# RG-LRU stage in a fixed order on three engines, with GpSimd's products and weight splits on VectorE and one convolution tap on ScalarE

## The chip, the cores and the metric

The kernel runs on 1 core of one Trainium2 chip. The time is device microseconds of one execution. Lower is better.

The engines are named as in the profile: PE is TensorE (matmuls), DVE is VectorE, ACT is ScalarE, POOL is GpSimd, SP is SyncE, whose queue issues most of the DMAs.

## The reference

A trunk of two layers over 128 prompt tokens and 1024 sample tokens (1152 columns in all, width 1024, inner width 2048). Layer 0 mixes by a Fourier transform, layer 1 by a bidirectional RG-LRU. The change touches layer 1, which is, cut to what matters:

```python
def _centred_dwconv(u, w, b):            # CONV_W = 4 taps per channel
    out = b
    for k in range(CONV_W):
        out = out + up[:, k:k + S] * w[k]

def _rglru_dir(u, w_r, b_r, w_i, b_i, lam, h0, reverse):
    r = sigmoid(_blockdiag(u, w_r) + b_r)          # 8 heads of 256 channels
    i = sigmoid(_blockdiag(u, w_i) + b_i)
    log_a = -LRU_C * r * softplus(-lam)
    a = exp(log_a)
    bterm = sqrt(-expm1(2.0 * log_a)) * (i * u)
    h = scan(a, bterm, reverse)                    # h[t] = a[t] h[t-1] + bterm[t]

def _layer(x, ...):
    u, z = split(h @ w_in, 2)
    uc = _centred_dwconv(u, conv_w, conv_b)
    y = _rglru_dir(uc, ..., False) + _rglru_dir(uc, ..., True)
    out = (y * silu(z)) @ w_out
    return x + gate * out
```

## The kernel before

The tokens lie along the free dimension, the channels on partitions, so the inner width is 16 channel tiles of 128, numbered m; two of them make one of the 8 heads, h. Every product is a float32 product made of three matmuls with rounded parts: high times high, high times low and low times high (`mm3`, L100 to L103). A float32 tile is split into such parts by `split` (L89): ACT casts the high part, and DVE or another engine subtracts it from the source for the low part. `wload` (L93) loads a 128 x 1024 tile of weights by SP's queue and splits it.

Stage H (from L798) runs over the heads. `stage_a` makes for both tiles of a head the projection u (three PSUM banks of 386, 384 and 388 columns, 24 matmuls each; ACT copies them to SBUF, L842), the convolution `uc` (the first tap with its bias on DVE, L847, then three more taps on DVE, L850) and its parts `uh` and `ul` (L852, recorded at L90 and L91). `stage_g` makes for one tile the two gates of both directions: 36 matmuls each tile and direction, tanh on ACT into `tr` and `ti` (L874), two more functions of `tr` into `nu` and `ga` (L878, L879), the square root (L882), then on DVE a run of products (L884 to L887), on POOL the product `ti*tr` (L888; on DVE in the last head), and on DVE the forward scan (L893), the backward scan (L897) and their sum (L902). POOL copies one column of each scan to `st`, the state that is an output. `z_mm` projects the gate branch z of a tile (72 matmuls) and makes z times its sigmoid in `szz` (L913 on ACT, L914 on DVE), and `z_out` multiplies it with the scans' sum (L919) and stores the result to `gD`, by SP's queue for the tiles up to 13 and by POOL's for 14 and 15. The low parts of the weights of this stage, and of the first weights of the stage after it, are made on POOL.

The output projection (`out_stage`, L682) reads `gD` again, as 16 tiles of 384 columns for each of three chunks (`g_load`, L609: the DMA into `gr`, then `gh` and `gl`), and multiplies it with `w_out`: 48 matmuls for each of 8 output tiles m. The `gr` tile of chunk 0 and channel tile 10 is written gr1010 in the order below, and so on; wo1020h is the high part of the first half of the weights of chunk 0 and output tile 2.

The order in which each engine gets its instructions isn't that of the source: the program is built with a list scheduler that simulates a timeline and places instructions by it. Each engine then works through its own list in order. In matmul order, a head goes: gates of its first tile, z of that tile, gates of its second tile, u of the two tiles of the next head, z of the second tile; then the next head's gates.

## Time and profile before

| | us |
|---|---|
| median of 3 runs | 1561.07 |
| lowest, highest | 1560.8, 1563.4 |
| span of the profiled execution | 1557.0 |
| PE busy | 1476.6 |
| DVE busy | 1105.8 |
| ACT busy | 744.8 |
| POOL busy | 443.3 |

The span is one execution on the hardware profiler, from its first to its last instruction; the time of a run is somewhat longer than the span. Busy times are sums over the instructions of one engine; a row that waits for another engine or for a DMA isn't counted. What counts for the time is the engine that is always busy and the waits of that engine.

### The profile page before, as it was taken

The page shows a single profiled execution, that of the slowest core. Times are in us where ns is not written, and L with a number is a line of the kernel's source. Part 1 is how long each engine was busy: PE and PEld are TensorE (multiplying, and loading weights), DVE is VectorE, ACT ScalarE, POOL GpSimd, SP SyncE. Part 2 cuts the span into 40 slices and gives each one's busy share as a digit, 9 for nine tenths or more (in the row PEclk, how much of TensorE's full clock was granted, in tenths as well). Part 3 has the DMA queues.
Part 4 walks back from the last instruction along what each step waited for, and adds up shares of the span by engine and source line. Part 5 has one row for each costly group of instructions (what it writes and reads, how often), then busy time and mean ns, then how long its engine had stood idle before and what let it go on. Part 6 is the DMA issues. An engine that isn't in the chain of part 4 may idle for free. (4 is left out here: it accounts for less than half of the span.)

```text
span 1557.0 us, 21619 instructions
## 1 busy us (share of the span) xinstructions
PE 1476.6 (95%) x8362; PEld 1426.1 (92%) x8362; DVE 1105.8 (71%) x1533; ACT 744.8 (48%) x1094; POOL 443.3 (28%) x285
## 2 busy tenths in 40 slices
PE   8879999999999999999699999999998999999997
PEld 5468999999999999999699898989898989899996
DVE  6995456898844677676968686868787787877453
ACT  7362334222223545348384746566573828554221
POOL 5676873000001011113434242515143432200000
PEclk9989999999999999999899999999999999999998
DMA  7523657877745665511111121211111111677451
GB/s 263 195 84 119 229 194 271 285 251 243 231 164 171 206 219 187 191 45 41 43 43 57 42 70 43 69 43 56 56 56 57 43 44 65 197 259 244 151 182 56
DMA packets 81625, 212.73 MB, mean 137 GB/s; under 512 B 9345, under 2 KB 40321, under 8 KB 81393
## 3 DMA queue, kind: packets, MB, share of 16 engines
q1 hardware_dynamic: 81170, 210.18, 40.5%
q8 instruction: 65, 1.06, 0.3%
q0 software_dynamic: 352, 1.18, 0.2%
q14 instruction: 38, 0.31, 0.1%
HBM read 171.98 MB, written 39.35 MB: 136 GB/s over the span
## 5 line engine op out<-in xcount | busy, mean ns | idle before, releaser
L439 POOL TENSOR_TENSOR xr<-xr,tab 128x384 f32<-128x384 f32 (+1 forms) x24 | 23.8, 994 | 365.2 <-DMA xr<-xT 357.6
L888 POOL TENSOR_TENSOR ti<-ti,tr 128x1156 f32<-128x1156 f32 x28 | 78.4, 2800 | 138.2 <-DVE ga L889 109.4
L887 DVE SCALAR_TENSOR_TENSOR ti<-ti,uc 128x1156 f32<-128x1156 f32 x32 | 57.6, 1802 | 63.1 <-ACT ti L874 63.1
L90 ACT CAST uh<-uc 128x1156 fp32r<-128x1156 f32 (+2 forms) x18 | 18.9, 1050 | 165.7 <-DVE uc L850 150.0
L133 DVE SCALAR_TENSOR_TENSOR sil1j<-wada,sil 128x1024 bf16<-128x1024 f32 x64 | 77.9, 1218 | 11.0 <-DMA wada<-w_ada 10.9
L884 DVE SCALAR_TENSOR_TENSOR nu<-ga,nu 128x1156 f32<-128x1156 f32 x32 | 60.9, 1902 | 22.4 <-ACT tr L882 22.3
L850 DVE SCALAR_TENSOR_TENSOR uc<-u,tab,uc 128x1156 f32<-128x1156 f32 (+2 forms) x54 | 75.8, 1405 | 1.1
L739 DVE SCALAR_TENSOR_TENSOR x<-o,ada,xr 128x128 f32<-128x128 f32 (+1 forms) x64 | 31.5, 512 | 55.4 <-PE o L103 54.5
L897 DVE TENSOR_TENSOR_SCAN nu<-ga,tab,ti 128x1155 f32<-128x1155 f32 x16 | 68.0, 4251 | 0.5
L90 ACT CAST gh<-gr 128x384 fp32r<-128x384 f32 x80 | 39.8, 511 | 55.6 <-DMA gr<-gD 55.2
L874 ACT ACTIVATE tr<-g,gb 128x386 f32<-128x386 f32 (+1 forms) x96 | 52.2, 582 | 21.8 <-PE g L103 21.7
L91 DVE TENSOR_TENSOR gl<-gr,gh 128x384 fp32r<-128x384 f32 x77 | 40.8, 554 | 29.7 <-ACT gh L90 29.5
L530 ACT CAST uh<-pu 128x256 fp32r<-128x256 f32 (+1 forms) x32 | 12.7, 398 | 89.3 <-PE pu L103 89.1
L531 DVE TENSOR_TENSOR ul<-pu,uh 128x256 fp32r<-128x256 f32 (+1 forms) x32 | 14.4, 452 | 54.5 <-ACT uh L530 54.4
L874 ACT ACTIVATE ti<-g,gb 128x386 f32<-128x386 f32 (+1 forms) x96 | 51.5, 582 | 0.0
L894 POOL COPY st<-nu 128x1 f32<-128x1 f32 x16 | 18.7, 1171 | 114.2 <-DVE nu L893 114.2
L879 ACT ACTIVATE ga<-tr,sm 128x1156 f32<-128x1156 f32 x32 | 43.3, 1352 | 3.3 <-DVE ga L889 3.3
L878 ACT ACTIVATE nu<-tr,sp2p 128x1156 f32<-128x1156 f32 x32 | 43.6, 1363 | 0.5
L886 DVE SCALAR_TENSOR_TENSOR tr<-ga,tr 128x1156 f32<-128x1156 f32 x32 | 43.2, 1351 | 0.6
L919 DVE SCALAR_TENSOR_TENSOR szz<-szz,nu 128x1155 f32<-128x1155 f32 x16 | 42.8, 2675 | 0.5
L646 ACT ACTIVATE sz<-z 128x384 f32<-128x384 f32 x48 | 22.9, 487 | 40.0 <-PE z L103 19.8
L882 ACT ACT_TABLE_LOAD x32 | 41.1, 1283 | 0.6
(1860 smaller groups left out, 5836.7 us busy)
## 6 DMA issues: line engine op xcount, KB each, us to landing
wo<-w_out SPq DMA_DIRECT2D x96, 512.0 KB, 4.4
wada<-w_ada SPq DMA_DIRECT2D x40, 512.0 KB, 4.2
wz<-w_z SPq DMA_DIRECT2D x32, 512.0 KB, 4.2
gr<-gD SPq DMA_DIRECT2D x80, 192.0 KB, 3.8
yD<-y SPq DMA_DIRECT2D x16, 576.0 KB, 5.2
zy<-yD SPq DMA_DIRECT2D x16, 576.0 KB, 6.6
wu<-w_u SPq DMA_DIRECT2D x16, 512.0 KB, 3.5
wg<-w_gate SPq DMA_DIRECT2D x16, 512.0 KB, 3.7
```

The costliest lines, as they stand in the source:

```text
L90: A.copy(hi, src)
L133: V.scalar_tensor_tensor(junk, w, 0.5, sil[:, q, :], op0=ALU.mult, op1=ALU.mult, accum_out=ada[:, layer, mt, q:q + 1])
L850: V.scalar_tensor_tensor(uc[:, lo:hi], u[:, lo + t:hi + t], convw[:, m, t:t + 1], uc[:, lo:hi], op0=ALU.mult, op1=ALU.add)
L874: A.activation(t[:, lo:hi], pt[:, 0:hi - lo], AF.Tanh, scale=0.5, bias=gb2[:, 2 * d + mat, m:m + 1])
L878: A.activation(nu, tr, AF.Tanh, scale=sp2[:, d, m:m + 1], bias=sp2[:, d, m:m + 1])
L879: A.activation(ga, tr, AF.Exp, scale=sm4[:, d, m:m + 1], bias=sm4[:, d, m:m + 1])
L884: V.scalar_tensor_tensor(nu, ga, 1.0, nu, op0=ALU.add, op1=ALU.mult)
L886: V.scalar_tensor_tensor(tr, ga, 1.0, tr, op0=ALU.add, op1=ALU.mult)
L887: V.scalar_tensor_tensor(ti, ti, 1.0, uc, op0=ALU.add, op1=ALU.mult)
L888: (PL if h < 7 else V).tensor_tensor(ti, ti, tr, op=ALU.mult)
L897: V.tensor_tensor_scan(nu[:, 0:L][:, ::-1], ga[:, 0:L][:, ::-1], ti[:, 0:L][:, ::-1], h0[:, 1, m:m + 1], ALU.mult, ALU.add)
L919: V.scalar_tensor_tensor(sz[:, 0:L], sz[:, 0:L], 0.5, y[:, 0:L], op0=ALU.mult, op1=ALU.mult)
```

## The change

In stage H, the order of PE, DVE and ACT is no longer left to the scheduler. The source is rewritten so that each operation is registered with a class `Plan`: its engine, an estimated cost, and the tiles that it reads and writes. `Plan.order` keeps PE's matmuls in the order in which they are registered, computes for every other operation a latest time from that, and then simulates a list schedule; `emit` issues the operations in that order, and the scheduler is told to keep it for these three engines. DMA issues of the stage are in the plan too, but SP and POOL still go by the scheduler.

With it go these edits: the low parts of the stage's weights are made on DVE (`lo` in `load`); the product `ti*tr` is on DVE in every head (`p5`); the first of the four taps, now the one with offset 2, is computed by ACT straight from PSUM, beside its copy (`tap` in `stage_u`), so that DVE has three taps left; the square roots of both directions of a tile stand together (`roots`); `szz` of tile 15 uses the one buffer of the tag `sz` like the others; and all stores of `gD` in layer 1 stand on SP's queue. The arithmetic is the same but for the order of the taps.

```diff
+        def load(src, name):
...
+            def lo():
+                T["lo", n] = wp.tile([128, 1024], F32R, tag="lo", name=name + "l", bufs=4)
+                V.tensor_tensor(T["lo", n], T["raw", n], T["hi", n].bitcast(F32), op=ALU.subtract)
...
+                def tap(p=p, lo=lo, hi=min(hi, GW)):
+                    A.activation(T["uc", m][:, lo:hi], T["ps", p][:, 0:hi - lo], AF.Identity, scale=convw[:, m, 2:3], bias=convb[:, m:m + 1])
...
-                    V.tensor_scalar(uc[:, lo:hi], u[:, lo:hi], convw[:, m, 0:1], convb[:, m:m + 1],
-                                    op0=ALU.mult, op1=ALU.add)
-                    for t in range(1, 4):
...
+            for t in (0, 1, 3):
+                P.add("DVE", c, lambda t=t: tap(t), r=[ut], w=[("uc", m)])
...
-            return [wload(a["w_gate"][h][:, d], f"wg{h}{d}", PL) for d in range(2)]
...
-            for tr, ti, nu, ga in tt:
-                A.activation(tr, nu, AF.Sqrt, scale=0.25)
+            def roots():
+                for n in ns:
+                    A.activation(T["tr", n], T["nu", n], AF.Sqrt, scale=0.25)
+            P.add("ACT", 4.9, roots, r=[("nu", n) for n in ns], w=[("tr", n) for n in ns])
...
-                (PL if h < 7 else V).tensor_tensor(ti, ti, tr, op=ALU.mult)
+                    V.tensor_tensor(ti, ti, T["tr", n], op=ALU.mult)
...
-            w = uw[2] if m == 0 else wload(a["w_z1"][m], f"wz1_{m}", PL)
-            sz = eb.tile([128, GW], F32, tag="tr" if m == MT - 1 else "sz", name=f"szz{m}", bufs=2 if m == MT - 1 else 1)
+                        T["sz", m] = eb.tile([128, GW], F32, tag="sz", name=f"szz{m}", bufs=1)
...
-            q = SY if m < MT - 2 else PL
-            q.dma_start(gD[1][m][:, 0:SP], sz[:, 0:SP])
-            q.dma_start(gD[1][m][:, SP:NT], sz[:, SP + GAP:L])
+                SY.dma_start(gD[1][m][:, 0:SP], T["sz", m][:, 0:SP])
+                SY.dma_start(gD[1][m][:, SP:NT], T["sz", m][:, SP + GAP:L])
...
+        with tc.manual_schedule(engines=ENG):
+            P.emit()
```

Over the whole program DVE has 1443 rows in place of 1399, ACT 1098 in place of 1082 (40 table loads among them in place of 72), POOL 213 in place of 290, SP 571 in place of 567. PE's 8252 rows stay, with some hundred of them in another place, at the start of head 0 and of each head.

First DVE, at the boundary from head 1 to head 2. The digits in `uc4` and `szz3` are the tile; those in `nu31`, `ga31`, `ti31` and `tr31` are the tile and the direction (1 is backward). Before:

```order
L897 SCALAR_TENSOR_TENSOR nu31_7941<-ga31_7942,tab_148,ti31_7892 128x1155
L847 TENSOR_SCALAR uc4_8054<-u4_7973,tab_148 128x1156
L902 TENSOR_TENSOR nu30_7887<-nu30_7887,nu31_7941 128x1155
L850 SCALAR_TENSOR_TENSOR uc4_8054<-u4_7973,tab_148,uc4_8054 128x1156 x3
L834 MEMSET u5_8069 128x2
L835 MEMSET u5_8069 128x1
L91 TENSOR_TENSOR ul4_8056<-uc4_8054,uh4_8055 128x1156
L847 TENSOR_SCALAR uc5_8150<-u5_8069,tab_148 128x1156
L850 SCALAR_TENSOR_TENSOR uc5_8150<-u5_8069,tab_148,uc5_8150 128x1156 x2
L914 SCALAR_TENSOR_TENSOR szz3_8165<-szz3_8165,zz30_8166 128x386
L850 SCALAR_TENSOR_TENSOR uc5_8150<-u5_8069,tab_148,uc5_8150 128x1156
```

The first row is the backward scan of tile 3, and the taps of uc4 and uc5 stand behind it. Of the same place now, in two pieces:

```order
L1084 SCALAR_TENSOR_TENSOR ti31_7986<-ti31_7986,uc3_7473 128x1156
L1074 SCALAR_TENSOR_TENSOR nu30_7880<-ga30_7992,nu30_7880 128x1156
L1016 SCALAR_TENSOR_TENSOR uc4_7771<-u4_7768,tab_148,uc4_7771 128x1156 x3
...
L944 TENSOR_TENSOR wg21l_8166<-wg21_7943,wg21h_8123 128x1024
L1026 TENSOR_TENSOR ul4_8193<-uc4_7771,uh4_8164 128x1156
L1016 SCALAR_TENSOR_TENSOR uc5_8156<-u5_8153,tab_148,uc5_8156 128x1156 x3
L1131 SCALAR_TENSOR_TENSOR szz3_8229<-szz3_8229,zz30_8168 128x386
L1088 TENSOR_TENSOR ti30_7898<-ti30_7898,tr30_7860 128x1156
...
L1026 TENSOR_TENSOR ul5_8237<-uc5_8156,uh5_8232 128x1156
```

The taps and `ul` of both tiles now stand ahead of both scans of tile 3, which follow further down; a weight split and the product `ti*tr` stand among them.

The second place is DVE at the end of the stage, where gated tile 15 (L919 before, L1138 now) is made while the output projection begins. Before:

```order
L890 MEMSET ti151_11768 128x3
L91 TENSOR_TENSOR gl103_11981<-gr103_11978,gh103_11980 128x384
L91 TENSOR_TENSOR gl104_11987<-gr104_11984,gh104_11986 128x384
L897 SCALAR_TENSOR_TENSOR nu151_11817<-ga151_11818,tab_148,ti151_11768 128x1155
L91 TENSOR_TENSOR gl105_11993<-gr105_11990,gh105_11992 128x384
L902 TENSOR_TENSOR nu150_11763<-nu150_11763,nu151_11817 128x1155
L91 TENSOR_TENSOR gl106_11999<-gr106_11996,gh106_11998 128x384
L91 TENSOR_TENSOR gl107_12005<-gr107_12002,gh107_12004 128x384
L919 SCALAR_TENSOR_TENSOR szz15_11849<-szz15_11849,nu150_11763 128x1155
```

And now:

```order
L1096 SCALAR_TENSOR_TENSOR nu150_11773<-ga150_11871,ti150_11791 128x1156
L186 TENSOR_TENSOR gl107_12038<-gr107_12035,gh107_12037 128x384
L1099 SCALAR_TENSOR_TENSOR nu151_11879<-ga151_11874,tab_148,ti151_11906 128x1155
L1131 SCALAR_TENSOR_TENSOR szz15_11938<-szz15_11938,zz151_11881 128x384
L186 TENSOR_TENSOR gl108_12044<-gr108_12041,gh108_12043 128x384
L186 TENSOR_TENSOR gl109_12050<-gr109_12047,gh109_12049 128x384
L1111 TENSOR_TENSOR nu150_11773<-nu150_11773,nu151_11879 128x1155
L1131 SCALAR_TENSOR_TENSOR szz15_11938<-szz15_11938,zz152_11910 128x386
L186 TENSOR_TENSOR wo1020l_12160<-wo1020_12157,wo1020h_12159 128x1024
L186 TENSOR_TENSOR wo1021l_12166<-wo1021_12163,wo1021h_12165 128x1024
L1138 SCALAR_TENSOR_TENSOR szz15_11938<-szz15_11938,nu150_11773 128x1155
```

The forward scan (nu150) stood well ahead of this place before and now stands directly ahead of the backward one, and two splits for the output projection and two weight splits have come ahead of the gated product.

The third place is SP's queue a little later, where the loads of the output projection and the last stores meet. Before:

```order
L95 DMA wo1031_12199<-w_out_1 128x1024
L622 DMA gr126_13314<-gD1_6_107 128x384
L95 DMA wo1040_12262<-w_out_1 128x1024
L622 DMA gr1010_12020<-gD1_10_111 128x384
L622 DMA gr1011_12026<-gD1_11_112 128x384
```

And now:

```order
L190 DMA wo1031_12232<-w_out_1 128x1024
L190 DMA wo1040_12295<-w_out_1 128x1024
L1141 DMA gD1_15_116<-szz15_11938 128x128
L1142 DMA gD1_15_116<-szz15_11938 128x1024
L717 DMA gr1010_12053<-gD1_10_111 128x384
L717 DMA gr1011_12059<-gD1_11_112 128x384
```

The two stores of gated tile 15, which were on POOL's queue, have come directly ahead of gr1010.

## Rows read from the trace of the kernel before

**Rows 1.** The page's first lines: the span, and each engine's busy time, share of the span and instructions.

```profile
span 1557.0 us, 21619 instructions
PE 1476.6 (95%) x8362; PEld 1426.1 (92%) x8362; DVE 1105.8 (71%) x1533; ACT 744.8 (48%) x1094; POOL 443.3 (28%) x285
```

**Rows 2.** PE's waits over the whole span: the waiting matmul's tile and line, the instruction that released it, the sum of such waits in us, how many, the longest.

```profile
PE g L101 <- ACT uh L90: 32.7, 9, 9.4
...
PE g L101 <- DVE szz L914: 4.1, 6, 0.8
```

**Rows 3.** Busy time of each engine in two stretches: the first is one head of stage H from its gates on, the second reaches from the end of the last z to the first matmul on channel tile 10 in the output projection. After the stretch stand its length and the busy us (and instructions) of PE, PEld, DVE, ACT and POOL, then the granted PE clock, the DMA share and GB/s.

```profile
778.00:861.85 83.85, 79.45 (x432) 78.52 (x432) 63.46 (x55) 50.36 (x65) 30.66 (x14) 0.97 0.16 52
...
1332.64:1360.05 27.41, 24.02 (x115) 20.63 (x115) 20.56 (x25) 10.30 (x18) 6.68 (x6) 0.94 0.68 215
```

**Rows 4.** PE's timeline, single matmuls at which a part of the work begins: start, duration, engine, line, operation, tiles; in brackets the idle time before it and its releaser. In order: a wait in the gates of head 0; the first matmul of u2; of u4; the first gate of head 2, and its next after the wait; the gates' other direction; z4, which follows it; the first matmul of the output projection; the first one on its channel tile 10.

```profile
722.87 0.44 PE L101 MATMUL g<-uh,wg01h 128*128 128x386 f32 x1 [2.13 <-ACT ti L874]
...
726.49 0.33 PE L101 MATMUL u<-h1h,wu_2h 128*128 128x386 f32 x1
...
819.37 0.35 PE L101 MATMUL u<-h1h,wu_4h 128*128 128x386 f32 x1
...
857.43 0.34 PE L101 MATMUL g<-uh,wg20h 128*128 128x386 f32 x1
...
861.85 0.57 PE L101 MATMUL g<-uh,wg20h 128*128 128x386 f32 x1 [3.72 <-ACT uh L90]
...
869.50 0.34 PE L101 MATMUL g<-uh,wg21h 128*128 128x386 f32 x1
...
875.93 0.35 PE L101 MATMUL zz<-h1h,wz_4h 128*128 128x386 f32 x1
...
1332.64 0.34 PE L101 MATMUL o<-gh,wo_0h 128*128 128x384 f32 x1
...
1360.05 0.34 PE L101 MATMUL o<-gh,wo_1h 128*128 128x384 f32 x1
```

**Rows 5.** The timelines of DVE, POOL and ACT at the boundary from head 1 to head 2, in order of time; the columns are those of rows 4.

```profile
838.73 2.40 POOL L91 TENSOR_TENSOR wg21l<-wg,wg21h 128x1024 fp32r<-128x1024 f32 x1
838.84 0.06 DVE L890 MEMSET ti<- 128x3 f32 x1 [2.79 <-POOL ti L888]
838.94 4.61 DVE L897 TENSOR_TENSOR_SCAN nu<-ga,tab,ti 128x1155 f32<-128x1155 f32 x1
...
845.51 4.33 DVE L850 SCALAR_TENSOR_TENSOR uc<-u,tab,uc 128x1156 f32<-128x1156 f32 x3
...
851.07 1.36 DVE L91 TENSOR_TENSOR ul<-uc,uh 128x1156 fp32r<-128x1156 f32 x1 [1.09 <-ACT uh L90]
...
852.87 2.41 POOL L91 TENSOR_TENSOR wz_4l<-wz,wz_4h 128x1024 fp32r<-128x1024 f32 x1 [8.51 <-ACT wz_4h L90]
853.15 2.75 DVE L847 TENSOR_SCALAR uc<-u,tab 128x1156 f32<-128x1156 f32 x1 [0.73 <-ACT u L842]
...
860.64 1.16 ACT L90 CAST uh<-uc 128x1156 fp32r<-128x1156 f32 x1 [5.72 <-DVE uc L850]
```

**Rows 6.** DVE's timeline in the last head: the product `ti*tr`, which is on DVE in that head alone, a backward scan, and a weight split.

```profile
1308.17 1.35 DVE L888 TENSOR_TENSOR ti<-ti,tr 128x1156 f32<-128x1156 f32 x1
...
1309.68 2.62 DVE L897 TENSOR_TENSOR_SCAN nu<-ga,tab,ti 128x1155 f32<-128x1155 f32 x1
...
1326.40 1.22 DVE L91 TENSOR_TENSOR wo1010l<-wo,wo1010h 128x1024 fp32r<-128x1024 f32 x1
```

**Rows 7.** Two stretches with the columns of rows 3: one right after a gate's wait, one in the output projection's first microseconds.

```profile
862.00:865.40 3.40, 3.40 (x11) 3.03 (x12) 3.37 (x4) 2.24 (x5) 2.20 (x1) 0.50 0.00 0
...
1336.40:1339.90 3.50, 3.36 (x10) 3.06 (x11) 3.50 (x4) 0.66 (x2) 2.17 (x2) 0.51 0.28 68
```

**Rows 8.** Groups of instructions: two from the six heads between 780 and 1280 us (line, engine, operation, tiles, shapes, count, busy us, mean ns, idle time before them), and the instructions of line 780 in the stage before (duration in ns: lowest, median, highest).

```profile
L847 DVE TENSOR_SCALAR uc<-u,tab 128x1156 f32<-128x1156 f32 x12 | 21.6, 1796 | 4.4 <-ACT u L842 4.4
...
L882 ACT ACT_TABLE_LOAD x24 | 30.8, 1283 | 0.4
...
L780 ACT ACTIVATE h1h<-x,coef x32: 386/556/622, 539.7 to 680.9; 128x384 fp32r<-128x384 f32 x16, 128x128 fp32r<-128x128 f32 x8, 128x256 fp32r<-128x256 f32 x8
```

**Rows 9.** The timelines of DVE and of SP's queue from the last scans of the stage into the output projection; the columns are those of rows 4. The row of SP at 1352.48 begins with the issue of gr1010, the last row with gl1010.

```profile
1322.57 0.76 DVE L885 TENSOR_SCALAR ga<-nu 128x1156 f32<-128x1156 f32 x1
...
1327.54 2.56 DVE L893 TENSOR_TENSOR_SCAN nu<-ga,ti 128x1156 f32<-128x1156 f32 x1
1330.02 1.33 DVE L887 SCALAR_TENSOR_TENSOR ti<-ti,uc 128x1156 f32<-128x1156 f32 x1
...
1339.57 0.54 DVE L914 SCALAR_TENSOR_TENSOR szz<-szz,zz 128x386 f32<-128x386 f32 x1
1340.05 0.55 DVE L91 TENSOR_TENSOR gl<-gr,gh 128x384 fp32r<-128x384 f32 x1
...
1346.19 1.35 DVE L919 SCALAR_TENSOR_TENSOR szz<-szz,nu 128x1155 f32<-128x1155 f32 x1
...
1352.48 2.07 SPq L622 DMA_DIRECT2D gr<-gD  x4
...
1358.94 2.08 DVE L91 TENSOR_TENSOR gl<-gr,gh 128x384 fp32r<-128x384 f32 x4 [2.87 <-ACT gh L90]
```

**Rows 10.** The page's list of DMA issues: tiles, queue, operation, count, KB each, median us from issue to landing.

```profile
gD<-szz SPq DMA_DIRECT2D x14, 512.0 KB, 3.5
```

More of the change, by code (lines that the diff above doesn't have):

```diff
@@ L823, in body @@
         st = ec.tile([128, 2, MT], F32, name="st")
-        def stage_a(h, early={}):
-            out = []
-            for i in range(2):
-                m = 2 * h + i
-                w = uw[m] if h == 0 else wload(a["w_u1"][m], f"wu1_{m}", PL)
+        P = Plan({"raw": 3, "hi": 4, "lo": 4, "u": 1, "uc": 3, "uh": 2, "ul": 2, "tr": 2, "ti": 3, "nu": 3, "ga": 2, "sz": 1, "ps": 8})
+        T = {}
+        wn = [3]
+        for n in range(3):
+            T["hi", n], T["lo", n] = uw[n]
+            P.given(("hi", n))
+            P.given(("lo", n))
@@ new lines, in body, with psum_ops, mm, wproj @@
+        pn = [0]
+        def psum_ops(name, mms, cost, reads):
+            n = pn[0]
+            pn[0] += 1
+            def mm():
+                T["ps", n] = ps(name)
+                mms(T["ps", n])
+            P.add("PE", cost, mm, r=reads, w=[("ps", n)])
+            return n
+        def wproj(n, name, lo, hi):
+            def mms(pt):
+                proj(pt, (T["hi", n], T["lo", n]), lo, hi)
+            return psum_ops(name, mms, 24 * (hi - lo + 32) / 2400, [("hi", n), ("lo", n)])
@@ L830, in stage_a, with given, stage_u, pads @@
+        def given(tile_):
+            n = pn[0]
+            pn[0] += 1
+            T["ps", n] = tile_
+            P.given(("ps", n))
+            return n
+        def stage_u(m, early=None):
+            n = None if m < 2 else load(a["w_u1"][m], f"wu1_{m}")
+            ut = ("nu", -1) if m == 1 else ("u", max(m - 1, 0))
+            def pads():
                 if m == 1:
-                    u = eb.tile([128, NG + 3], F32, tag="nu", name=f"u{m}", bufs=3)
+                    u = T[ut] = eb.tile([128, NG + 3], F32, tag="nu", name=f"u{m}", bufs=3)
@@ L832, in stage_a @@
                 else:
[L833 removed]
+                    u = T[ut] = ea.tile([128, NG + 3], F32, tag="u", name=f"u{m}", bufs=1)
                 V.memset(u[:, 0:2], 0.0)
                 V.memset(u[:, NG + 2:NG + 3], 0.0)
[L836 to L842 removed]
@@ new lines, in stage_u, with cp @@
+            P.add("DVE", 0.12, pads, w=[ut, ("uc", m)])
+            for c, (lo, hi) in enumerate(HC):
+                if (m, c) in early_n:
+                    p = early_n[m, c]
+                elif m < 2:
+                    p = psum_ops(f"u{m}{c}", lambda pt, lo=lo, hi=hi: proj(pt, uw[m], lo, hi), 24 * (hi - lo + 32) / 2400, [("hi", m), ("lo", m)])
+                else:
+                    p = wproj(n, f"u{m}{c}", lo, hi)
+                def cp(p=p, lo=lo, hi=hi):
+                    A.copy(T[ut][:, 2 + lo:2 + hi], T["ps", p][:, 0:hi - lo])
+                def tap(p=p, lo=lo, hi=min(hi, GW)):
+                    A.activation(T["uc", m][:, lo:hi], T["ps", p][:, 0:hi - lo], AF.Identity, scale=convw[:, m, 2:3], bias=convb[:, m:m + 1])
+                P.add("ACT", 0.48, cp, r=[("ps", p)], w=[ut])
+                P.add("ACT", 0.55, tap, r=[("ps", p)], w=[("uc", m)])
+                if m < 2 and c == 1:
+                    conv(m, ut, 0, hi - 1)
@@ new lines, in z_out, with gated, store @@
+        def z_out(m):
+            def gated():
+                sz = T["sz", m]
+                V.scalar_tensor_tensor(sz[:, 0:L], sz[:, 0:L], 0.5, T["nu", 2 * m][:, 0:L], op0=ALU.mult, op1=ALU.mult)
+            def store():
+                SY.dma_start(gD[1][m][:, 0:SP], T["sz", m][:, 0:SP])
+                SY.dma_start(gD[1][m][:, SP:NT], T["sz", m][:, SP + GAP:L])
+            P.add("DVE", 1.36, gated, r=[("nu", 2 * m)], w=[("sz", m)])
+            P.add("SP", 0.2, store, r=[("sz", m)], lat=5.0)
@@ new lines, in body @@
+        early_n = {k: given(t) for k, t in early.items()}
+        gw = gweights(0)
+        stage_u(0)
+        stage_u(1)
+        for h in range(8):
+            if h == 0:
+                stage_z(0)
+            stage_g(h, gw, 0)
+            if h > 0:
+                stage_z(2 * h)
+            z_out(2 * h)
+            stage_g(h, gw, 1)
+            if h + 1 < 8:
+                stage_u(2 * h + 2)
+                stage_u(2 * h + 3)
+            stage_z(2 * h + 1)
+            z_out(2 * h + 1)
+            if h + 1 < 8:
+                gw = gweights(h + 1)
```

276 lines of the change are left out of this document (198 added, 78 removed).

## The prediction

> **What bounds the kernel now.** I first read the busy times: PE, the tensor engine, works 1476.6 of the span's 1557.0 us, and the next engine, DVE, 1105.8 [rows 1]. So only what makes PE wait, or slows its clock, can give time back. The list of PE's waits names what there is in the stage that the change rewrites (stage H, RG-LRU): 32.7 us in nine waits of gate matmuls for ScalarE's cast `uh`, and 4.1 us for the product on `szz` [rows 2]. The table of stretches shows one head: 83.85 us, PE busy for 79.45 of them, at a mean clock of 0.97 [rows 3].
>
> What would a head take if PE never waited? PE's own rows tell. u4, u5 and z3, 72 matmuls each, run from 819.37 to 857.43, or 12.69 us each; the 36 gate matmuls of one tile and direction run from 869.50 to 875.93, 6.43 us [rows 4]. A head is four of the former and four of the latter: 76.5 us.
>
> Next, why the gates wait. A timeline of the other engines across the boundary from head 1 to 2 shows a chain [rows 5]. DVE stands idle for 2.79 us until GpSimd's product `ti*tr` arrives; the backward scan of tile 3 follows, 4.61 us beside a GpSimd split; only then come the conv taps of uc4, its cast `uh`, the first tap of uc5 at 2.75 us beside another split, the other taps, and its `uh` at 860.64. PE restarts at 861.85, after 3.72 us [rows 4]. Two things make the chain late: the order (the taps of the new head stand behind the scan of the old one, and that behind GpSimd), and a stretch of DVE's rows beside GpSimd. Where GpSimd was quiet the same scan took 2.62 us, and the product, on DVE itself, 1.35 us [rows 6]. After the restart the granted clock is 0.50 (1.2 of 2.4 GHz) for 3.4 us, so 1.7 us more are lost [rows 7].
>
> **The change part by part.** *Waits removed in stage H.* From the start of u2 (726.49) to the end of z15 (1332.64) lie 606.2 us [rows 4]. The PE work in it is 14 u and 15 z parts of 12.69 us and 28 gate parts of 6.43 us, 368.0 + 180.0 = 548.0 us; the matmuls and nearly all of their order stay. If no boundary waits, **58.1 us** go. That hangs on three engines keeping up:
>
> *DVE.* It was busy for 63.46 us of a head [rows 3]. It gains six weight splits at 1.22 us (7.3) and four products at 1.35 us (5.4) [rows 6], and loses two first taps, 21.6/12 = 1.8 us each (3.6) [rows 8]. Without any relief that makes 72.6 us; if only the two backward scans of a head shrink, from 4.61 to 2.62, 68.6. Both stay below 76.5, so DVE isn't the bound by volume; what matters is whether the chain at the boundary is in time. The new order puts the taps of uc4 and uc5 ahead of the old head's scans. Counted from the start of u4, u5's last bank is full at 2 x 12.69 = 25.4 us. Its copy and its new tap on ScalarE end near 26.7, three DVE taps (4.33 us [rows 5]) at 31.0, the cast (1.16 us [rows 5]) at 32.2; DVE has two short rows more in that time (some 1.9 us at most, a `szz` or `ga` row and a product), and `ul5` takes 1.36 us [rows 5]: 34.6. PE needs it when z3 is over, at 3 x 12.69 + 0.3 = 38.4. The slack is about 4 us, so I take no wait.
>
> *ScalarE.* It was busy for 50.36 us of a head [rows 3]. The tap that it takes over is not in the trace: three activations from PSUM a tile. The nearest row is an Identity on 128 x 384 and less, 386 to 622 ns [rows 8]; three are 1.2 to 1.9 us a tile, I take the upper end, 3.7 us a head. Rooting both directions together removes four table loads of a head, 4 x 30.8/24 = 5.1 us [rows 8]. The pair now waits until both directions have their `nu`, and what stands behind it on ScalarE, the later copies of the new u, waits with it; eight PSUM banks cover that for PE. ScalarE ends below where it was.
>
> *GpSimd.* Its products and splits in the stage are gone and two one-column copies a tile are left, so it hardly overlaps with DVE.
>
> *The start.* The gates of head 0 now wait for two more splits on DVE (2 x 1.22 us), while the wait of 2.13 us at 722.87 [rows 4] can go: -2.1 to +2.4 us, I take +0.5. For short waits that may stay (buffers of `ga`, `tr`, `nu` that come free just in time) I add 1.0, between 0 and the 4.1 us that `szz` cost [rows 2].
>
> *The tail, where something is given back.* In the output projection the first ten channel tiles are loaded early; the eleventh, gr1010, waits. Before, the last gated product ended at 1347.54, 14.9 us after z15; gr1010 was issued at 1352.48 and its split began at 1358.94 [rows 9]; PE came to it at 1360.05 [rows 4], 27.4 us after z15, having been busy for 24.0 of them [rows 3]. Now two things differ. Both stores of tile 15, which stood on GpSimd's queue, stand on SP's, directly ahead of gr1010, which so can't be issued before the last gated product is over. And that product is later: from the last `ti` product with uc15 on (begun at 1330.02, 2.6 us ahead of z15's end, before [rows 9]; 2.2 ahead by my count of the new order), the new order has on DVE eight products of 1.35 us, two `ga` rows of 0.76, scans of 2.56 and 2.62, three `szz` rows of 0.55, seven `gl` splits of 0.55 and three weight splits of 1.22 [rows 6, 9]: 10.8 + 1.5 + 5.2 + 1.6 + 3.9 + 3.7 = 26.7, with the small fills 27. That ends 25 us after z15, with a wait or two for `gr` loads 26. From gr1010's issue to its split passed 6.46 us [rows 9], the split is 0.55, the store's two issues some 0.7: PE begins tile 10 some 34 us after z15, with no other work in order. So 34 - 27.4 = **6.6 us** are given back; the ends are 30 us (no `gr` waits, a quicker landing) and 38 (slower loads), that is 2.6 to 10.6.
>
> One rule speaks to the clock in this tail. First the rows: at 1336.4 to 1339.9 PE was granted 0.51 though it was busy for 3.36 of 3.5 us, and after the wait of 2.13 us at 722.87 it stayed at 1.00 [rows 4, 7]. The Trainium skill (TensorE: Matmul & The Clock Gate, "Why this matters for your kernels") lays a throughput drop in mid-kernel to idle gaps between bursts of matmuls; by that, a tail broken into short pieces costs no clock, while the first of these rows says that it may. While PE waits for tile 10 a slow clock costs nothing; it would cost if it lasted beyond. The row's price is half of 3.4 us, 1.7, which I take as nothing and keep for the range.
>
> **Sum.** 1557.0 - 58.1 + 0.5 + 1.0 + 6.6 = 1507.0 us of span. The time outside the span, 1561.07 (the median) - 1557.0 = 4.07 us, stays: **1511 us**. Its own range, with the ends of tail, start and clock, is 1505 to 1518.
>
> **The rivals.** *The tail is free* (0.10): the rows between the scans are short, the loads land early and nothing is lost after z15: 1511.0 - 6.6 = 1504.4, 1502 to 1505. Against it stands the store ahead of gr1010.
>
> *A part of each boundary wait remains* (0.16): the slack of 4 us is eaten, by taps from PSUM that take twice as long, by the paired roots holding ScalarE while the new u is ready, or by DVE rows that don't shrink. Waits of 1 to 2.5 us at seven boundaries, with 1.7 us of half clock at the longer ones, make 7 to 29 us: 1518 to 1540. For it: the 3.72 us of before ended a chain of the same kind.
>
> *The stretch is not GpSimd's* (0.05): the scan keeps 4.6 us, DVE has 72.6 us a head in a fixed order, and the chain is late at each boundary as now. Little is left of the 58.1 us: 1545 to 1562. Against it: the scan of 2.62 us [rows 6].
>
> *Slower* (0.06): `szz` has one buffer. ScalarE's tanh into it, at its fixed place, waits until the former tile's store has read it; everything behind it on ScalarE, the tanh of the gates above all, waits too, and PE runs out of PSUM banks. By my count the store is issued some 11 us ahead of that tanh, and such a store landed in 3.5 us [rows 10]. It decides when a store is held up behind a weight load on SP's queue: a buffer free only 23 us after the gated product would cost more than the 7.4 us that a head gains (58.1 over 606.2/76.5 = 7.9 heads), and the kernel is at 1562 or above. All but two of the stores stood on that queue before, which speaks against it.
>
> **How the numbers follow.** Forecast 0.63, free tail 0.10, remaining waits 0.16, stretch 0.05, slower 0.06. The range is 1502 to 1528: it leaves out the upper half of the remaining waits (0.08) and the last two cases (0.11). Within 0.2%, about what a measurement of this kernel can tell from no change, lies 1558 to 1564: the upper part of the stretch case, 0.02. Faster 0.92, slower 0.06.
>
> **What would show it.** Right: no wait of gate matmuls for `uh` above 0.5 us; heads of 76.5 us at clock 1.00; backward scans of 2.6 us throughout; DVE busy for 62 to 69 us a head; z15 over near 1276; in the output projection PE waiting for `gh` or `gl` of tile 10 until some 34 us after that. Wrong: a long wait in DVE's or ScalarE's fixed order behind which ready work stands, PE without free banks, or a store that is late on SP.

## The result, and the profile after

The changed kernel takes 1509.85 us (median of 4 runs, 1507.78 to 1511.16) where the kernel before took 1560.93 in the same session: a ratio of 0.9669, 95% interval 0.9655 to 0.9683. That is 1.2 us from the forecast of 1511 and inside its range. The profiled execution has a span of 1506.0 us. Below, PE is at line 196 to 198 where it was at 101 to 103, and `split` at 185 and 186 where it was at 90 and 91.

The page's first lines, which answer to [rows 1]:

```profile
span 1506.0 us, 21530 instructions
PE 1462.0 (97%) x8362; PEld 1418.6 (94%) x8362; DVE 1084.6 (72%) x1588; ACT 738.6 (49%) x1110; POOL 229.1 (15%) x208
```

PE's waits from 690 to 1400 us (stage H and what follows it), which answer to [rows 2]:

```profile
PE o L197 <- DVE gl L186: 4.4, 3, 1.8
PE o L196 <- ACT gh L185: 2.6, 1, 2.6
PE o L197 <- POOL gl L186: 0.9, 1, 0.9
...
PE g L196 <- ACT ti L1053: 0.6, 1, 0.6
```

Of the gate matmuls (`g`) one waits for 0.6 us, and one for 0.2 us that is not shown, both in head 0; before, they had waited for 32.7 us on `uh`. What is left are waits of the output projection (`o`). Two stretches, in the columns of [rows 3]: a head from u4 to u6, and the time from the end of z15 to the first matmul on channel tile 10.

```profile
800.52:877.00 76.48, 76.48 (x433) 76.45 (x433) 62.85 (x63) 51.13 (x69) 6.52 (x6) 1.00 0.18 57
1272.07:1308.84 36.77, 27.77 (x115) 24.75 (x115) 29.63 (x34) 11.76 (x21) 5.77 (x5) 0.81 0.55 172
```

A head takes 76.48 us and PE is busy in all of it, at full clock. DVE works for 62.85 us of it, less than the 63.46 before, though it has six splits and four products more and only two taps less: its rows are shorter. The second row is the price: 36.77 us where it was 27.41.

The boundary from head 1 to 2 in DVE's timeline, which answers to [rows 5]:

```profile
822.64 1.22 DVE L944 TENSOR_TENSOR wg21l<-wg,wg21h 128x1024 fp32r<-128x1024 f32 x1
823.98 1.36 DVE L1026 TENSOR_TENSOR ul<-uc,uh 128x1156 fp32r<-128x1156 f32 x1
827.18 4.34 DVE L1016 SCALAR_TENSOR_TENSOR uc<-u,tab,uc 128x1156 f32<-128x1156 f32 x3 [1.84 <-ACT u L999]
831.44 0.55 DVE L1131 SCALAR_TENSOR_TENSOR szz<-szz,zz 128x386 f32<-128x386 f32 x1
...
833.50 1.35 DVE L1026 TENSOR_TENSOR ul<-uc,uh 128x1156 fp32r<-128x1156 f32 x1
```

The second `ul` is over at 834.85, 34.3 us after u4's start at 800.52, and PE needs it after 838.59.

Every kernel's profile, those of the experiments too, can be cut at two matmuls: the first of u2, and the last of z15 (its end taken 0.17 us after its start, which is the step from one matmul to the next). The time is the median of the runs; the three columns behind it come from the profiled execution and add up to its span. In us:

| kernel | time | start to u2 | u2 to end of z15 | end of z15 to end of span |
|---|---|---|---|---|
| before | 1560.93 | 726.5 | 606.2 | 224.4 |
| changed | 1509.85 | 724.0 | 548.0 | 233.9 |
| order alone | 1551.55 | 736.7 | 581.5 | 232.2 |
| moves alone | 1504.47 | 727.2 | 548.2 | 224.8 |
| order, GpSimd's work back | 1568.28 | 732.7 | 598.9 | 233.7 |
| tap back on VectorE | 1516.13 | 731.6 | 548.0 | 234.3 |
| product alone | 1533.77 | 726.7 | 578.7 | 224.6 |
| splits alone | 1518.61 | 731.4 | 561.6 | 225.3 |
| stores back on GpSimd's queue | 1512.94 | 727.2 | 548.0 | 235.6 |
| roots of tile 15 apart | 1506.89 | 725.8 | 548.0 | 231.2 |
| product and splits | 1509.86 | 730.9 | 550.7 | 225.8 |
| gl on GpSimd | 1510.15 | 726.0 | 548.0 | 234.8 |
| hybrid | 1502.75 | 724.6 | 548.3 | 227.0 |
| hybrid, tail's edits undone | 1501.42 | 725.6 | 548.2 | 226.6 |

Single numbers of the first column carry some 3 us that aren't the change's: the first gate matmul, ahead of which the compared kernels hardly differ, came at 697.0 to 700.3 us. The second column repeats to a few tenths. The 51.0 us between the spans of the first two rows are 2.4 + 58.1 - 9.5.

One row of the table matters more than the others: the moves alone, in the scheduler's own order, are 5.4 us faster than the changed kernel, and their interval (0.9623 to 0.9652, below) doesn't touch that of the change.

### The profile page after: what moved, and what is told of

It is laid out like the page before. It is cut to its first block, busy times and chain, and to the rows that moved or that the text cites. A ratio compares the mean times of both kernels' runs of the same rounds, so it can differ in the third digit from the quotient of the medians.

```text
span 1506.0 us, 21530 instructions
## 1 busy us (share of the span) xinstructions
PE 1462.0 (97%) x8362; PEld 1418.6 (94%) x8362; DVE 1084.6 (72%) x1588; ACT 738.6 (49%) x1110; POOL 229.1 (15%) x208
## 4 chain that ended last, share of the span: by engine, by line
PE 48%; DVE 2%; ACT 1%; issue 1%; DMA 1%; POOL 0%; DVEq 0%; POOLq 0%; ACTq 0%
PE o L198 4%; PE o L196 4%; PE o L197 4%; PE u L198 4%; PE u L196 4%; PE u L197 4%; PE g L196 4%; PE zz L196 4%; PE zz L198 4%; PE zz L197 4%; PE g L197 4%; PE g L198 4%; DMA gr<-gD 1%; DVE nu L1099 0%; POOL gl L186 0%
## 5 line engine op out<-in xcount | busy, mean ns | idle before, releaser
L228 DVE SCALAR_TENSOR_TENSOR sil1j<-wada,sil 128x1024 bf16<-128x1024 f32 x64 | 78.0, 1219 | 10.8 <-DMA wada<-w_ada 10.6
L1016 DVE SCALAR_TENSOR_TENSOR uc<-u,tab,uc 128x1156 f32<-128x1156 f32 (+2 forms) x54 | 69.2, 1288 | 20.5 <-ACT u L999 19.1
L1097 POOL COPY st<-nu 128x1 f32<-128x1 f32 x16 | 10.4, 648 | 434.0 <-DVE nu L1096 433.7
L1074 DVE SCALAR_TENSOR_TENSOR nu<-ga,nu 128x1156 f32<-128x1156 f32 x32 | 43.5, 1359 | 45.3 <-ACT tr L1070 45.3
L1053 ACT ACTIVATE tr<-g,gb 128x386 f32<-128x386 f32 (+1 forms) x96 | 55.4, 585 | 25.6 <-PE g L198 21.3
L1002 ACT ACTIVATE uc<-u,tab 128x386 f32<-128x386 f32 (+1 forms) x48 | 32.4, 674 | 60.8 <-PE u L198 60.8
L1127 ACT ACTIVATE szz<-zz 128x386 f32<-128x386 f32 (+1 forms) x48 | 23.6, 495 | 74.7 <-PE zz L198 74.5
L1084 DVE SCALAR_TENSOR_TENSOR ti<-ti,uc 128x1156 f32<-128x1156 f32 x32 | 42.9, 1357 | 9.6 <-ACT ti L1053 9.3
L1099 DVE TENSOR_TENSOR_SCAN nu<-ga,tab,ti 128x1155 f32<-128x1155 f32 x16 | 43.9, 2745 | 0.1
L1088 DVE TENSOR_TENSOR ti<-ti,tr 128x1156 f32<-128x1156 f32 x32 | 43.4, 1356 | 0.3
L1096 DVE TENSOR_TENSOR_SCAN nu<-ga,ti 128x1156 f32<-128x1156 f32 x16 | 40.9, 2555 | 0.4
```

The source lines that it names most:

```text
L228: V.scalar_tensor_tensor(junk, w, 0.5, sil[:, q, :], op0=ALU.mult, op1=ALU.mult, accum_out=ada[:, layer, mt, q:q + 1])
L1016: V.scalar_tensor_tensor(T["uc", m][:, lo:hi], T[ut][:, lo + t:hi + t], convw[:, m, t:t + 1], T["uc", m][:, lo:hi], op0=ALU.mult, op1=ALU.add)
L1053: A.activation(T[tg, n][:, lo:hi], T["ps", p][:, 0:hi - lo], AF.Tanh, scale=0.5, bias=gb2[:, 2 * d + mat, m:m + 1])
L1074: V.scalar_tensor_tensor(T["nu", n], T["ga", n], 1.0, T["nu", n], op0=ALU.add, op1=ALU.mult)
L1088: V.tensor_tensor(ti, ti, T["tr", n], op=ALU.mult)
L1099: V.tensor_tensor_scan(nu[:, 0:L][:, ::-1], ga[:, 0:L][:, ::-1], ti[:, 0:L][:, ::-1], h0[:, 1, m:m + 1], ALU.mult, ALU.add)
```

## The experiments

The first question is which of the parts removes the boundary waits. Two theories: the order (the conv taps stood behind the old head's scans), or GpSimd (DVE waited for its product, and was stretched beside it).

**Order alone.** Edit, beside the stores and the square roots as before:

```diff
-                V.tensor_tensor(T["lo", n], T["raw", n], T["hi", n].bitcast(F32), op=ALU.subtract)
+                PL.tensor_tensor(T["lo", n], T["raw", n], T["hi", n].bitcast(F32), op=ALU.subtract)
...
-                P.add("ACT", 0.55, tap, r=[("ps", p)], w=[("uc", m)])
...
+                        PL.tensor_tensor(T["ti", n], T["ti", n], T["tr", n], op=ALU.mult)
```

> The planned order alone: the weight splits and the products ti*tr of heads 0 to 6 back on GpSimd, the first tap back on VectorE from SBUF, the square roots apart, the stores of tiles 14 and 15 back on GpSimd's queue; the planner knows of all that by their costs. Theory 'order' (the gates waited because the conv taps stood behind the old head's scans): most of the gain stays, 1508 to 1520 us. Theory 'GpSimd' (they waited because DVE waited for GpSimd's product and was stretched beside it): more than half of the gain is gone, 1535 us or more, with scans of 4.6 us and waits of gate matmuls for uh or ul of 2 us and more at each boundary.

1551.55 us, ratio 0.9940 (0.9925 to 0.9955). In stage H the order alone wins 24.7 of the 58.1 us, and it loses 10.2 us before u2 and 7.8 in the tail. A wait of 2.7 us stays at each boundary but the first, which has 8.6 us; it is now mostly on `ul`:

```profile
PE g L197 <- DVE ul L1023: 23.7, 9, 4.7
PE g L196 <- ACT uh L1018: 9.4, 2, 6.1
```

At the boundary from head 1 to 2 the backward scan takes 2.62 us, not the expected 4.6; there it is three taps that are long, 8.65 us, beside GpSimd's product and a split.

**Moves alone.** The kernel before with `PL` replaced in the stage's splits and in the product, and the tap on ScalarE:

```diff
-                (PL if h < 7 else V).tensor_tensor(ti, ti, tr, op=ALU.mult)
+                V.tensor_tensor(ti, ti, tr, op=ALU.mult)
...
-            return [wload(a["w_gate"][h][:, d], f"wg{h}{d}", PL) for d in range(2)]
+            return [wload(a["w_gate"][h][:, d], f"wg{h}{d}") for d in range(2)]
...
+                    A.activation(uc[:, lo:min(hi, GW)], pt[:, 0:min(hi, GW) - lo], AF.Identity, scale=convw[:, m, 2:3], bias=convb[:, m:m + 1])
```

> The kernel before with the moves and without the planned order: weight splits and products ti*tr on VectorE, one tap on ScalarE from PSUM, the scheduler's own order. Theory 'GpSimd': the idle time of 2.8 us for the product, 2.0 us of the scan and 1.9 us of the first tap go out of a chain that was 3.7 us late, so most of the gain is there, 1508 to 1522 us. Theory 'order': the scans still stand among the taps and DVE has about 9 us more to do in a head, so the gates still wait 2 to 4 us at each boundary, 1535 to 1560 us.

1504.47 us, ratio 0.9638 (0.9623 to 0.9652), with no planned order at all. A head and the tail, as above:

```profile
804.09:880.57 76.48, 76.48 (x434) 76.45 (x434) 64.13 (x66) 53.46 (x71) 3.96 (x4) 1.00 0.20 65
1275.46:1303.38 27.92, 22.95 (x115) 19.44 (x115) 21.06 (x26) 10.70 (x19) 6.76 (x6) 1.00 0.70 212
```

The head is the same 76.48 us, and the tail is as short as before. At the boundary from head 1 to 2 the scan still stands among the taps of uc4 (one ahead of it, two behind), but its rows have their short lengths:

```profile
822.83 1.42 DVE L850 SCALAR_TENSOR_TENSOR uc<-u,tab,uc 128x1156 f32<-128x1156 f32 x1
...
824.16 2.62 DVE L897 TENSOR_TENSOR_SCAN nu<-ga,tab,ti 128x1155 f32<-128x1155 f32 x1
826.70 1.39 DVE L850 SCALAR_TENSOR_TENSOR uc<-u,tab,uc 128x1156 f32<-128x1156 f32 x1
```

So the planned order isn't needed to remove the waits, and by itself it wins back less than half of what they cost. The scheduler's order isn't quite that of before either (no tap stood ahead of the scan there): it simulates again after every edit, so each run of this kind moves rows too.

**Order, with GpSimd's work given back** (tap and paired roots kept):

```diff
-                V.tensor_tensor(T["lo", n], T["raw", n], T["hi", n].bitcast(F32), op=ALU.subtract)
+                PL.tensor_tensor(T["lo", n], T["raw", n], T["hi", n].bitcast(F32), op=ALU.subtract)
...
+                        PL.tensor_tensor(T["ti", n], T["ti", n], T["tr", n], op=ALU.mult)
```

> The changed kernel with only GpSimd's work given back: weight splits, and the products ti*tr of heads 0 to 6, on GpSimd; tap on ScalarE, paired square roots and planned order kept. Theory 'order': 1506 to 1515 us, no wait of gates above 1 us. Theory 'GpSimd': 1530 us or more.

1568.28 us, ratio 1.0050 (1.0033 to 1.0067): half a per cent slower than the kernel before. Timelines of DVE and POOL at the boundary from head 1 to 2:

```profile
832.52 8.49 DVE L1016 SCALAR_TENSOR_TENSOR uc<-u,tab,uc 128x1156 f32<-128x1156 f32 x3
...
842.67 2.56 DVE L1097 TENSOR_TENSOR_SCAN nu<-ga,ti 128x1156 f32<-128x1156 f32 x1
842.76 4.94 POOL L1109 TENSOR_TENSOR ti<-ti,tr 128x1156 f32<-128x1156 f32 x1 [4.44 <-DVE tr L1080]
...
845.14 3.78 DVE L1026 TENSOR_TENSOR ul<-uc,uh 128x1156 fp32r<-128x1156 f32 x1
848.98 2.62 DVE L1100 TENSOR_TENSOR_SCAN nu<-ga,tab,ti 128x1155 f32<-128x1155 f32 x1
851.52 6.48 DVE L1016 SCALAR_TENSOR_TENSOR uc<-u,tab,uc 128x1156 f32<-128x1156 f32 x3
```

Three taps take 8.49 and 6.48 us in place of 4.34, `ul` 3.78 in place of 1.36. A fixed order doesn't take the stretch away; it lays it on other rows, here the taps that the chain needs. Why this kernel is 17 us slower than the order alone, which lacks the tap on ScalarE and the paired roots among others, no run separates.

**The tap given back** (four DVE taps in the planned order):

```diff
+                V.tensor_scalar(T["uc", m][:, lo:hi], T[ut][:, lo + 2:hi + 2], convw[:, m, 2:3], convb[:, m:m + 1], op0=ALU.mult, op1=ALU.add)
```

> The changed kernel with only the tap given back: the first of four taps on VectorE from SBUF, planned again. DVE has two rows of 0.85 us more in a head, and the chain to ul is 0.85 us longer where 4 us were spare, so both theories say no change, 1508 to 1513 us. A third theory, that the tap on ScalarE carries the gain, says 1525 us or more.

1516.13 us, ratio 0.9712 (0.9696 to 0.9727), above the range of both theories. The heads stay at 76.48 us, as they said; the loss is at the start, where the first gates wait 3.0 us for the split `wg00l`, and some 3 us lie ahead of the first gate, where the runs vary by as much.

The second question: product or splits? Each alone, in the kernel before.

**Product alone:**

```diff
-                (PL if h < 7 else V).tensor_tensor(ti, ti, tr, op=ALU.mult)
+                V.tensor_tensor(ti, ti, tr, op=ALU.mult)
```

> The kernel before with one move: the product ti*tr on VectorE in every head; the weight splits stay on GpSimd, the taps on VectorE, the order the scheduler's. Theory 'wait' (of GpSimd's work it is DVE's idle time for the product that makes the chain late): the 2.8 us before the scan go and 1.35 us of work come, the boundary waits fall below 2 us, 1520 to 1535 us. Theory 'stretch' (it is the longer rows of DVE beside the splits): nearly nothing is won, 1550 to 1562 us.

**Splits alone**, of `wu1` and `wz1` as of `wg`:

```diff
-            return [wload(a["w_gate"][h][:, d], f"wg{h}{d}", PL) for d in range(2)]
+            return [wload(a["w_gate"][h][:, d], f"wg{h}{d}") for d in range(2)]
```

> The kernel before with one move: the stage's weight splits on VectorE; the products stay on GpSimd, the taps on VectorE, the order the scheduler's. Theory 'stretch': the scan falls from 4.6 to 2.6 us and the first tap from 2.75 to 0.85, one or two splits of 1.22 come into the chain, 1520 to 1540 us. Theory 'wait': DVE still stands idle for the product and has 7.3 us a head more to do, 1555 to 1575 us.

The product alone gives 1533.77 us, ratio 0.9826 (0.9812 to 0.9840); the splits alone 1518.61, ratio 0.9730 (0.9716 to 0.9743). One head of each, the product's first:

```profile
855.63:935.30 79.67, 78.12 (x432) 77.52 (x432) 67.11 (x59) 50.28 (x65) 19.40 (x10) 0.98 0.17 55
```

```profile
935.00:1011.50 76.50, 76.50 (x434) 76.33 (x433) 60.91 (x59) 49.91 (x64) 16.66 (x8) 1.00 0.17 58
```

With the splits moved, the heads from the fourth on are already free of waits, though GpSimd still makes the products. In stage H the product alone wins 27.5 us of the 58.1, the splits alone 44.6; together that is more than there is, so the two overlap. They can't be read as the shares of "wait" and "stretch", because each edit mends some of the other's part: with the product alone the backward scans are down to 2.62 us too, and with the splits alone DVE no longer stands idle for the product, as the scheduler has put the first tap of uc4 into that time (beside the product it takes 3.24 us).

**Product and splits, without the tap** (both edits above in one kernel):

```diff
-                (PL if h < 7 else V).tensor_tensor(ti, ti, tr, op=ALU.mult)
+                V.tensor_tensor(ti, ti, tr, op=ALU.mult)
...
-            return [wload(a["w_gate"][h][:, d], f"wg{h}{d}", PL) for d in range(2)]
+            return [wload(a["w_gate"][h][:, d], f"wg{h}{d}") for d in range(2)]
```

> The kernel before with two moves and no more: products ti*tr and weight splits on VectorE; four taps on VectorE, no planned order. If the two moves off GpSimd make the gain, the boundary waits are gone and the time is 1503 to 1512 us. If the tap on ScalarE is needed beside them in the scheduler's order (it takes 1.7 us a head off DVE), waits of 1 to 3 us stay at the boundaries, 1515 to 1530 us.

1509.86 us, ratio 0.9685 (0.9669 to 0.9700): 550.7 us from u2 to z15, so one wait of 1.7 us is left, at the first boundary, and one of 0.4 for `szz`. The tap on ScalarE is worth that and some 2 us at the start.

The third question is the tail. My theory was the store ahead of gr1010; the rival, that the splits `gl` stand behind the late products of tile 15 on DVE.

**Stores back on GpSimd's queue:**

```diff
+                q = SY if m < MT - 2 else PL
```

> The changed kernel with one thing undone: the stores of tiles 14 and 15 on GpSimd's queue, so that no store stands ahead of gr1010 on SP's. Theory 'store' (the prediction's: the tail is long because tile 10 can't be loaded before the last store is issued): tile 10's split comes 5 us or more earlier and the time falls by 4 to 7 us, 1503 to 1506 us. Theory 'chain' (the tail is long because the first splits gl103 to gl107 stand behind the late products and scans of tile 15 on DVE, with half clock after each wait): PE reaches tile 10 no earlier, 1508 to 1511 us.

1512.94 us, ratio 0.9689 (0.9675 to 0.9703), above both ranges; the tail didn't shrink. But the question wasn't put cleanly: without the stores, a third weight load moved ahead of gr1010 on SP's queue, which held it until 1308.21, 33.0 us after z15 in place of 29.5.

**Square roots of tile 15 apart:**

```diff
-            P.add("ACT", 4.9, roots, r=[("nu", n) for n in ns], w=[("tr", n) for n in ns])
+            for g in ([(n,) for n in ns] if m == 15 else [ns]):
```

> The changed kernel with one thing undone: in tile 15 alone the square roots of the two directions stand apart, two table loads more, so that the forward direction's products and scan are over before the last z and not behind it; planned again, which puts the gated product of tile 15 ahead of gl106. Theory 'chain': the waits on gl fall and the gated product ends some 8 us earlier, 1501 to 1506 us, with PE at tile 10 some 28 to 31 us after z15. If the tail is long because the loads gr100 to gr107 themselves come late, it stays at 1508 to 1511 us.

1506.89 us, ratio 0.9652 (0.9639 to 0.9666). The tail is 2.7 us shorter, not 4 to 9: the gated product came 9.5 us earlier, but the output projection's first matmul now waits:

```profile
1279.36 0.69 PE L196 MATMUL o<-gh,wo_0h 128*128 128x384 f32 x1 [5.40 <-ACT gh L185]
```

That cast, of gh100, had its load by 1276.43 and was held until DVE had read uc15 for the last time, in the second `ti` product:

```profile
1278.79 0.51 ACT L185 CAST gh<-gr 128x384 fp32r<-128x384 f32 x1 [2.00 <-DVE ti L1085]
```

The same row holds the second load, gr101, here, in the kernel before and in the changed one. Of the latter, SP's waits from 1255 to 1315 us:

```profile
SPq L717 <- DVE ti L1084: 2.3, 1, 2.3
```

I take it that the output projection's tiles lie where the stage's tiles lay. In this run that row had moved behind the forward scan. gr101 was issued at 1331.38 in the kernel before, 1.3 us ahead of z15's end; at 1273.18 in the changed one, 1.1 us behind it; at 1278.79 here, 5.0 us behind it. In the changed kernel no matmul waited for it, though.

**Low parts gl100 to gl109 on GpSimd:**

```diff
-            gt[0, k] = gt0.get(k) if layer == 0 else g_load(layer, 0, k, None, PL if k in (0,1,2) else V)
+            gt[0, k] = gt0.get(k) if layer == 0 else g_load(layer, 0, k, None, PL if k < 10 else V)
```

> The changed kernel with one thing more: the low parts of the first ten gated tiles of the output projection (gl100 to gl109) on GpSimd, which is idle there, in place of three. Theory 'chain' (splits stand behind tile 15's products on DVE): PE's waits on gl fall from 5.3 to below 3 us and the raw buffers come free earlier, 1505 to 1508 us. Theory 'loads' (the loads gr101 and following can't start before the last reader of uc15 on DVE, whatever engine splits): no change, 1508 to 1511 us.

1510.15 us, ratio 0.9680 (0.9667 to 0.9693): no change. It doesn't decide between the theories, though: PE's waits didn't fall, they only changed their engine.

```profile
PE o L197 <- POOL gl L186: 5.4, 6, 1.9
...
1276.74 11.28 POOL L186 TENSOR_TENSOR gl<-gr,gh 128x384 fp32r<-128x384 f32 x6 [13.17 <-ACT gh L185]
```

GpSimd needs 11.28 us for six of these splits, DVE 0.55 for one; and beside them the rows of tile 15 on DVE are stretched again (a `ti*tr` product 2.15 us in place of 1.35, the backward scan 3.29 in place of 2.62).

**Hybrid**, the planned order up to the last head, then the scheduler's:

```diff
-            P.emit()
+            for i in seq[:cut]:
+                P.ops[i]["fn"]()
+        for i in seq[cut:]:
+            P.ops[i]["fn"]()
```

> The changed kernel with the planned order up to the first gate of the last head; from there on the scheduler sets the order as it did before. If the tail's 9 us are the planned order's (both gate directions of tile 15 in parallel on DVE and ScalarE, so that the rows that free the buffers for gr come late), they go and what is left is 1500 to 1503 us, the fastest of all; if the tail is long for the moves' sake, it stays at 1508 to 1511 us.

1502.75 us, ratio 0.9636 (0.9622 to 0.9649). gr101 is issued 1.6 us ahead of z15's end again, the gated product ends 14.7 us behind it (28.6 in the changed kernel), and the tail is 227.0 us. The stores of tile 15 still stand on SP's queue here.

**Hybrid with the tail's two edits undone:**

```diff
-                        T["sz", m] = eb.tile([128, GW], F32, tag="sz", name=f"szz{m}", bufs=1)
+                        T["sz", m] = eb.tile([128, GW], F32, tag="tr" if m == MT - 1 else "sz", name=f"szz{m}", bufs=2 if m == MT - 1 else 1)
...
+                q = SY if m < MT - 2 else PL
```

> The kernel of the run before (planned order up to the last head, then the scheduler's) with two more edits of the change undone: the stores of tiles 14 and 15 on GpSimd's queue, szz of tile 15 in a buffer of tr. If these two hold the 2.3 us that its tail was still longer than the tail of the kernel before (223.6 in place of 221.3 us from the end of z15 to the end), the time is 1499 to 1502 us; if they don't matter, 1501 to 1504 us.

1501.42 us, ratio 0.9626 (0.9613 to 0.9639): the lowest median of all, and faster than the changed kernel beyond both intervals, but not to be told from the hybrid (0.9622 to 0.9649) or the moves alone (0.9623 to 0.9652). Its tail is 0.4 us shorter than the hybrid's, too little to tell whether these edits matter. (Counted as in the table, the two tails that the expectation compares are 227.0 and 224.4 us.)

## Why the prediction was right, and where it wasn't

*The sum.* 1511 for 1509.85 is closer than its terms were: the tail cost 2.9 us more than forecast, the start 2.9 less, and of the 1.0 us for short waits nothing came. That these cancel is luck. So is it that the 4.07 us "outside the span" did no harm: it is a median less the span of one execution. In the changed kernel the profiled execution took 1507.78 us with a span of 1506.0, so 1.8 us lie outside, and the rest of the difference of 3.85 is that this execution was the quickest of the four.

*What bounds.* Right. PE bound, with the boundary waits to be won; the 58.1 us of stage H came out at 58.1 (606.2 to 548.0), and heads at 76.48.

*Why the gates waited.* I named two causes, the order and the stretch beside GpSimd, and asked the planned order to make room. **This step was half wrong.** The moves alone remove the waits in the scheduler's order; the order alone leaves 33.5 of the 58.1 us, and with the tap and the paired roots but GpSimd at work 50.9. What the order does add is slack: `ul` was ready 34.3 us after u4's start, by my count 34.6, while with the moves alone the same row ends at 843.27, when PE has begun the gates at 842.15 with at most 0.2 us to wait. The kernel didn't need that slack.

*DVE.* Right that it isn't the bound: 62.85 us a head, below both of my bounds, since not only the scans shrink. Of the 16 backward scans 15 took 2.60 to 2.62 us, and one, in the last head, 4.69 beside a split on GpSimd. In the run with GpSimd's work back three taps took 8.49 us in place of 4.34, while the `szz` product, one of whose inputs is in PSUM, took 0.53 to 0.56 us in all 48 rows, some of them beside GpSimd. The Trainium skill (SBUF — State Buffer, "Who interferes with whom") says that an instruction of VectorE with two inputs in SBUF contends with one of GpSimd that reads SBUF, and that one with at most one such input, outside the 2-port modes, does not. These rows agree. Rows with a single tensor input were stretched too, the first tap (2.75 us [rows 5], and 0.88 in the run with product and splits moved) and `ga` (3.14 us in the run with GpSimd's work back, and 0.76 in the changed kernel); whether they ran in such a mode no run here shows.

*ScalarE.* The tap from PSUM was mis-sized a little: 650 to 730 ns where I had taken 622. No gate waited for it, and over the span ScalarE's busy time fell from 744.8 to 738.6 us.

```profile
L1002 ACT ACTIVATE uc<-u,tab x48: 650/674/730, 682.7 to 1208.5; 128x386 f32<-128x386 f32 x32, 128x384 f32<-128x384 f32 x16
```

*The start.* I allowed +0.5 and it gained 2.4, of which 1.9 lie between the first gate and u2 (28.94 to 27.03 us, by the same matmuls). This is the one place where the order pays: with the moves alone it is 30.3, with the hybrid 27.0.

*The tail.* The size held (9.4 to tile 10, within 2.6 to 10.6, for 6.6); **the mechanism held only in part**, so the size is partly luck. Tile 10 did come late: the gated product ended at 1300.66, 28.6 us after z15 where I had 26, and tile 10's split began 35.4 us after z15.

```profile
1299.31 1.35 DVE L1138 SCALAR_TENSOR_TENSOR szz<-szz,nu 128x1155 f32<-128x1155 f32 x1
...
1307.48 2.06 DVE L186 TENSOR_TENSOR gl<-gr,gh 128x384 fp32r<-128x384 f32 x4 [2.61 <-ACT gh L185]
```

But PE didn't stand waiting for it; it reached tile 10 at 1308.84 with other work up to that moment. Of the 9.4 us, 5.6 are idle time from earlier on (9.0 us before tile 10 where it was 3.4), for the first loads and splits; the rest is the clock (below):

```profile
1274.80 0.49 PE L196 MATMUL o<-gh,wo_0h 128*128 128x384 f32 x1 [2.56 <-ACT gh L185]
1276.47 0.69 PE L197 MATMUL o<-gl,wo_0h 128*128 128x384 f32 x1 [0.85 <-POOL gl L186]
1284.15 0.44 PE L197 MATMUL o<-gl,wo_0h 128*128 128x384 f32 x1 [1.82 <-DVE gl L186]
1291.52 0.44 PE L197 MATMUL o<-gl,wo_0h 128*128 128x384 f32 x1 [1.37 <-DVE gl L186]
1294.96 0.44 PE L197 MATMUL o<-gl,wo_1h 128*128 128x384 f32 x1 [1.25 <-DVE gl L186]
```

The first of these waits is for gr100. It stands on SP's queue behind a weight load that is held until DVE has made `wo1010l`, and DVE made that 3.4 us ahead of z15's end where it had been 6.2; so gr100 was issued 1.7 us ahead of z15's end where it had been 4.6. The last three are for gl103, gl107 and gl108, which stood on DVE behind the rows of tile 15. gl103, for one, had its cast (the first row) 4.3 us before it was split (the second):

```profile
1278.79 0.51 ACT L185 CAST gh<-gr 128x384 fp32r<-128x384 f32 x1 [0.84 <-DMA gr<-gD]
...
1283.55 1.48 DVE L186 TENSOR_TENSOR gl<-gr,gh 128x384 fp32r<-128x384 f32 x3
```

So two chains of nearly equal length ended there, the gated product with its store and load, and the first loads and splits; the edits that were meant to reach one of them shortened the tail by 2.7 us at most. What sets both is the planned order of the last head, where both directions of tile 15 run side by side; handing that head back to the scheduler took 7 of the 9.5 us. The stores stayed ahead of gr1010 in that run, and PE reached tile 10 some 28.7 us after z15: a store on SP's queue costs little where the gated product is early (0.4 us between the last two runs, which differ in it). I had looked at the one load behind the store and not at the first loads and splits. Which share each chain has in the changed kernel is not settled, since the store was never taken away with gr1010's place kept, and the splits were never taken off DVE without GpSimd beside it.

*The clock in the tail.* I took it as nothing. PE was busy for 27.77 us with the 115 matmuls that took 22.95 us at clock 1.00 in the run of moves alone and 24.02 before: 3.75 us of the 9.4 are longer matmuls, that is clock (a mean of 0.81 in place of 0.94). In the stretch

```profile
1295.50:1299.00 3.50, 3.27 (x11) 2.76 (x10) 3.50 (x4) 0.00 (x0) 0.00 (x0) 0.51 0.35 112
```

PE is at half clock though it is busy for 3.27 of 3.5 us, and its waits just before were short (1.37 and 1.25 us the longest). With the moves alone the same part, with waits of up to 1.25 us, kept 1.00; and in the kernel before the clock stayed at 1.00 around the single wait of 2.13 us in head 0, a row that the prediction named and [rows 7] doesn't show:

```profile
722.00:729.00 7.00, 6.04 (x33) 5.72 (x34) 5.82 (x7) 5.93 (x9) 2.54 (x2) 1.00 0.20 66
```

What decides between these cases is not shown. The Trainium skill's rule on idle gaps (TensorE: Matmul & The Clock Gate, "Why this matters for your kernels") would have given no loss in the tail; the trace doesn't bear that out.

*The rivals.* The tail was not free, and no boundary wait remained. The stretch was GpSimd's, as forecast. No store held `szz`; the one wait of a gate matmul that may be for a bank is the 0.6 us for ScalarE's tanh, in head 0.
